# Sums of squares of query, key and head tiles as two float32r matmuls in place of one float32 matmul

## The chip, the cores and the metric

One core of one Trainium2 chip runs the whole program. The metric is the device time of one execution in microseconds. Three runs of the kernel before are given, and one more execution was profiled.

## What is computed

Two layers of a hybrid trunk over 128 context rows and 256 latent rows, 1024 wide. The rows lie side by side as 384 columns on the chip; the model dimension lies on the partitions.

```python
# layer l: x += 0.5*g1*FFN(norm(x)); x += g2*Mixer_l(norm(x)); x += 0.5*g3*FFN(norm(x))
def rmsnorm(x, g):
    return x * lax.rsqrt(jnp.mean(x * x, axis=-1, keepdims=True) + EPS) * g
# even mixer: two-way RG-LRU beside differential attention (4 heads, q and k of 2 x 64)
q = rmsnorm(q.reshape(B, S, 4, 2, 64), q_g);  k = rmsnorm(k.reshape(B, S, 4, 2, 64), k_g)
w = softmax(q0 k0) - lam * softmax(q1 k1)
o = rmsnorm(w @ v, subln_g) * (1 - lam_init)          # over 128 elements of a head
# odd mixer: windowed grouped attention with sinks, 16 query heads, 4 key heads of 64
q = rmsnorm(q.reshape(B, S, 4, 4, 64), q_g);  k = rmsnorm(k.reshape(B, S, 4, 64), k_g)
```

Each `rmsnorm` over a head needs the sum of squares over 64 or 128 partitions of a tile. It is had by a matmul with a constant matrix: `bones` (two blocks of 64 by 64 with 1/64) for q and k tiles, which hold two rows of 64 each, and `ones_h` (1/128 everywhere) for a head of the even mixer.

## The kernel before, in words

A dense product is made of three float32r matmuls per 128x128 weight tile (`mm3`): the high part of the weights with the high and the low part of x, and the low part of the weights with the high part of x, all into one PSUM tile. The weights come in order through SP's queue into `raw`; each is split into `hi` (a copy, as a rule on ACT) and `lo` (a subtraction on DVE), 1024 columns at a time, four deep.

The order of the instructions is written by a small planner. `Clock` keeps a rough time for each engine; the matmul stream (projections, FFN, output projection) is written straight through, and after each matmul `Sched.tick` lets side chains, which are generators, write their next stage when by that clock their inputs are there. A `yield` names the conditions of the next stage: tiles, events, free PSUM banks (`msb`, `scb`, `mmb`), or an engine that is idle (`DVE_IDLE`). Each engine then works through its own list in order. `copy` picks ACT, or DVE where by the clock DVE is done 0.5 us earlier. Constants of this planner (`WIDE_E`, `O_EARLY`, `XN_O` and so on) stay as they are.

A mixer runs in this order. `proj_pass` writes the projection tiles: in the even mixer four `xr` tiles (whose chains feed the RG-LRU scans on DVE), then q, k and v of each of four heads, then four `gt` tiles (gelu gates of the RG-LRU); in the odd mixer twice k, v and four q tiles. Each q or k tile starts `q_chain` or `k_chain`, both through `qk_norm`: square on ACT, a wait for the squares and a PSUM bank, the matmul with `bones`, Ln and Exp on ACT (the inverse root), multiplication on DVE, two DMAs that swap rotary pairs, and the rotation on DVE. `a_chain` makes scores, softmax and transposes for a block of 128 queries, `o_chain` the product with v; in the even mixer `o_chain` then squares its result, sums with `ones_h`, normalises and splits it (`split_out`). Then `out_pass` writes the output projection in two parts of K tiles for each of eight output tiles: in the even mixer first the four heads, then the four RG-LRU tiles; in the odd mixer first K tiles 0 to 2, then 3 to 7. Two PSUM tiles are open at first, two more once all heads are ready. After the last part of an output tile, `update` and `prep` (DVE and ACT) ready it for the next FFN.

Tiles of 384 columns come from one pool, `slab`, of 79. The constants: `cst` holds the cosines, the sines and `bones`, loaded by one DMA from SP's queue at the start; `mixer_consts` is a chain that works out further small constants beside the first FFN.

Of the kernel before, what the change touches and what calls it, by code (L numbers as in the profile page):

```python
# [11 lines left out]
F32 = mybir.dt.float32  # L12
F32R = mybir.dt.float32r
BF16 = mybir.dt.bfloat16
AF = mybir.ActivationFunctionType
ALU = mybir.AluOpType
AX = mybir.AxisListType
PSUM = bass.MemoryType.PSUM

P = 128  # L20
NP_, NS = 128, 256
T = NP_ + NS
# [25 lines left out]
class Event:  # L48
    """Something that a chain of instructions has still to emit, with the tiles that it leaves."""

# [4 lines left out]
class Banks:  # L55
    """PSUM tiles of one tag: how many may be in use at a time, and when the free ones fell free."""

# [4 lines left out]
class Idle:  # L62
    """Ready when an engine has nothing else queued."""

# [18 lines left out]
class Clock:  # L83
    """Rough times of the engines while the program is written: they order the emission and nothing else."""

# [33 lines left out]
class Sched:  # L119
    """Emits the stages of side chains between pieces of the matmul stream, each when its inputs should be there."""  # L120

# [80 lines left out]
class Eng:  # L202
    """An engine's instructions, timed by the clock as they are written."""

# [49 lines left out]
def emit(tc, D, order):  # L254
    nc = tc.nc
    ctx = ExitStack()
    with ctx:
        pool = lambda n, b, **k: ctx.enter_context(tc.tile_pool(name=n, bufs=b, **k))
        cpool = pool("const", 1)
# [10 lines left out]
        clock = sched.clock  # L270
# [51 lines left out]
        def copy(out, in_, scale=None):  # L322
            """out = in_ (times a column), on the engine that should be done with it first."""
            k = {} if scale is None else {"scale": scale}
            r = max(clock.at(in_)[0], clock.at(out)[0])
            ta = max(clock.free["ACT"], r) + S_.cost("activation", out, [in_], k)
            td = max(clock.free["DVE"], r) + V.cost("tensor_copy", out, [in_] if scale is None else [in_, scale], k)
            if td + ON_ACT < ta:
                if scale is None:
                    V.tensor_copy(out, in_)  # L330
                else:
                    V.tensor_scalar(out, in_, scale, None, ALU.mult)
            else:
                act(out, in_, AF.Copy, **k)

# [1 line left out]
        scT = cpool.tile([P, KD, 32], F32, name="scT")  # L337
# [13 lines left out]
        cos, sin = cst[:, 0:256], cst[:, 256:512]  # L351
        bones = cst[:, 512:640]
        ident = cpool.tile([P, P], F32, name="ident")
# [4 lines left out]
        V.memset(ones_d, 1.0 / 1024)  # L358
        ones_h = cpool.tile([P, P], F32, name="ones_h")
        V.memset(ones_h, 1.0 / 128)  # L360
        kc = cpool.tile([P, 4], F32, name="kc")
# [8 lines left out]

# [1 line left out]
        class WS:  # L372
# [70 lines left out]
        def mm(ps, lhsT, rhs, start=True, stop=True):  # L443
            TE.matmul(ps, lhsT=lhsT, rhs=rhs, start=start, stop=stop)
            sched.tick()

# [1 line left out]
        M = {}  # L448
# [27 lines left out]
        def mod_one():  # L476
            """Generator: one modulation tile, a condition per stage."""
            i = mod_at[0]
            l, k, t = mod_todo[i]
            mod_at[0] += 1  # L480
            if t == 0:
                M[l, k] = cpool.tile([P, 8, 2], F32, name=f"M{l}_{k}")
            w = mod_tiles.pop(i)
            for c in range(2):
                yield DVE_IDLE, w
                junk = modp.tile([P, 1024], BF16, tag="junk", name=nm("junk"), bufs=1)
                V.tensor_tensor_reduce(out=junk, in0=w, in1=cbc[:, c, :], scale=1.0, scalar=0.0,
                                       op0=ALU.mult, op1=ALU.add, accum_out=M[l, k][:, t, c:c + 1])
            mod_load()
            if t == 7:  # L490
                mod_finish(l, k)
                mod_done.add((l, k))
# [19 lines left out]

# [1 line left out]
        class XS:  # L514
# [7 lines left out]
        def prep(d, with_sh=True):  # L522
            """Generator: scaled x as two float32r parts, and the sum of squares."""
            q = sl()
            hi = XS.hi[d] = sl(F32R, TB)
            lo = XS.lo[d] = sl(F32R, TB)
            act(q, x[d], AF.Square)
            for r, c in RANGES:
                copy(hi[:, r], x[d][:, r], XS.A[:, d, c:c + 1])
            if with_sh:  # L530
                copy(hi[:, T:TB], XS.sh[:, d, :])
            yield hi, q
            if XS.sq is None:
                XS.sq = q
            else:
                V.tensor_tensor(XS.sq, XS.sq, q, ALU.add)
            for r, c in RANGES:
                V.scalar_tensor_tensor(lo[:, r], x[d][:, r], XS.A[:, d, c:c + 1], r32(hi[:, r]), ALU.mult, ALU.subtract)
            if with_sh:
                V.tensor_tensor(lo[:, T:TB], XS.sh[:, d, :], r32(hi[:, T:TB]), ALU.subtract)  # L540
            sched.fire(XS.ev[d], hi, lo, XS.sq)
# [18 lines left out]
        def normed_all(low):  # L560
            """Starts the chains that leave the normed and modulated x as two float32r parts."""
            xn = [None] * KD
# [37 lines left out]

# [1 line left out]
        def ffn(l, n, nxt):  # L602
# [82 lines left out]

# [1 line left out]
        def evac(ps, direct):  # L687
# [26 lines left out]
        def qk_norm(t, bc, gate, gs):  # L714
            """Generator: leaves the normed rows in t, then returns the two parts of the rotated ones."""
            sq = sl()
            if bc is None:
                act(sq, t, AF.Square)
            else:
                for r, c in RANGES:  # L720
                    act(sq[:, r], t[:, r], AF.Square, bias=bc[:, c:c + 1])
            yield (sq, msb) if gate is None else (sq, msb, gate)
            ps = mst()
            mm(ps[:, :T], bones, sq)
            act(sq, ps[:, :T], AF.Ln, bias=c_eps)
# [16 lines left out]
            V.tensor_tensor(sq[:, 0:NS], sq[:, 0:NS], sin, ALU.mult)  # L742
            return u, sq

        def q_chain(ps, direct, gate, gs, out):
# [77 lines left out]
        def transposed(src, n):  # L823
            """w (128 queries, n*128 keys) -> SBUF (keys, n, queries)."""
            pt = mst()
            for b in range(n):
                TE.transpose(pt[:, b * P:(b + 1) * P], src[:, b * P:(b + 1) * P], ident)
            w = sl()
            copy(w[:, :n * P], pt[:, :n * P])
            free(msb, pt, w)  # L830
            return w
# [15 lines left out]
        def proj_pass(tiles, key, done, low):  # L847
            """Projection tiles in order; the first two share a K order that leaves the last tile of x late."""
            i = 0
# [31 lines left out]
        def out_pass(key, gm, nxt, ready, free_at, early, wide):  # L881
            """Output projection. The K tiles in `early` come first: x takes their part while the others are computed."""
            prep_begin(*nxt)
# [7 lines left out]
            def slot(t, ps):  # L891
                """A bank that has nothing to do: kept while there are units to come."""
                if todo:
                    slots.append((t, ps))
                else:
                    (msb if ps.tensor.name in borrowed else mmb).at.append(t)
# [63 lines left out]

# [1 line left out]
        def even_mixer(nxt):  # L962
# [160 lines left out]
            def o_chain(h):  # L1123
# [12 lines left out]
                free(msb, po, og)  # L1136
                yield sq, msb
                ps = mst()
                mm(ps[:, :T], ones_h, sq)
                act(sq, ps[:, :T], AF.Ln, bias=c_eps)  # L1140
# [29 lines left out]

# [1 line left out]
        def odd_mixer(nxt):  # L1172
# [69 lines left out]

# [1 line left out]
        def wm_load(i):  # L1244
# [5 lines left out]
        def mixer_consts():  # L1250
            yield RS.ev, el, pp
            # differential lambda, negated
            V.tensor_scalar(gsub, par("subln"), 1.0 - LAM_INIT, None, ALU.mult)
            lj = sl()
            for m in range(2):
                V.tensor_tensor_reduce(out=lj[:, 0:64], in0=el[:, 2 * m, :], in1=el[:, 2 * m + 1, :], scale=1.0, scalar=0.0,
                                       op0=ALU.mult, op1=ALU.add, accum_out=ls[:, m:m + 1])
            # -8 * softplus(-lam) on (128, 2 directions, 4 tiles); log1p by its series in z / (2 + z)
            lam = pp[:, PPC["lam"][0]:PPC["lam"][0] + 8]
# [89 lines left out]

# order of the 64 rows of a q or k head on the partitions: the two rows of a rotary pair side by side  # L1350
ROPE = np.array([b + i + s for b in (0, 32) for i in range(16) for s in (0, 16)])
# [135 lines left out]
```

## Time and profile before

| | us |
|---|---|
| median of 3 runs | 1466.14 |
| the runs | 1464.9, 1466.14, 1466.73 |
| the profiled execution, first to last instruction (its span) | 1464.2 |
| PE busy in it | 1436.7 |
| PEld (weight loads, beside PE) | 1398.4 |
| DVE busy | 1115.4 |
| ACT busy | 659.8 |
| POOL busy | 103.8 |

The profiled execution has no other time than its span; the median of the runs is 1.9 us above that. Busy time of PE is modelled to the drain of each matmul, so a short gap between two matmuls does not show in it. The even mixer's matmuls run from about 318 to 482 us, the odd mixer's from about 1042 to 1188 us; the FFNs take the rest.

### The profile page before, as it was taken

To read this page: it belongs to the slowest core of one execution; us is meant where nothing else is said; L and a number is where in the kernel's file an instruction comes from. 1 tells how busy PE (TensorE), PEld (TensorE's weight loads), DVE (VectorE), ACT (ScalarE), POOL (GpSimd) and SP (SyncE) were. 2 spreads that over 40 slices of the span, in tenths; PEclk is the share of its full clock that TensorE was granted. 3 is DMA by queue.
4 is the path that set the end of the run, shared out by engine and by line. 5 is a ranking of instruction groups with operands and counts; after the bars stand their busy time and mean duration, and the time that the engine had idled before them with its cause. 6 is when DMAs were issued, how large, how long until landed. Compare 5 with 4: busy or idle time off the path is not lost.

```text
span 1464.2 us, 21823 instructions
## 1 busy us (share of the span) xinstructions
PE 1436.7 (98%) x8354; PEld 1398.4 (96%) x8354; DVE 1115.4 (76%) x2103; ACT 659.8 (45%) x1193; POOL 103.8 (7%) x214
## 2 busy tenths in 40 slices
PE   4999999999999999999999999999999999999998
PEld 1999999998889999999999999999998899999998
DVE  3899999969998998999979997444698795444332
ACT  3643333348875633333345333333477664333321
POOL 0001111110220011111100110000100000000000
PEclk9999999999999999999999999999999999999999
DMA  9557767652322366766744766333331233333430
GB/s 361 216 185 257 246 245 257 235 173 101 120 99 97 140 230 236 254 243 231 254 177 153 251 243 196 135 119 130 117 107 51 77 120 115 133 126 116 146 135 22
DMA packets 49560, 250.67 MB, mean 171 GB/s; under 512 B 6464, under 2 KB 10960, under 8 KB 28336
## 3 DMA queue, kind: packets, MB, share of 16 engines
q1 hardware_dynamic: 29664, 180.05, 34.0%
q0 software_dynamic: 19792, 69.23, 14.2%
q8 instruction: 66, 1.08, 0.3%
q14 instruction: 38, 0.31, 0.1%
HBM read 244.53 MB, written 2.36 MB: 169 GB/s over the span
## 4 chain that ended last, share of the span: by engine, by line
PE 95%; DMA 2%; DVE 2%; ACT 1%; issue 0%; SPq 0%; DVEq 0%; ACTq 0%
PE sc L214 54%; PE mm L214 36%; PE ms L214 5%; DVE s L214 1%; DMA wm<-in_wm 1%; DMA s<-in_xT 1%; DMA raw<-in_wst 0%; DVE lo L214 0%; ACT s L214 0%; DMA s<-s 0%; ACT hi L214 0%; ACT L317 0%; SPq L737 0%; SPq L1296 0%; DVEq L1434 0%
## 5 line engine op out<-in xcount | busy, mean ns | idle before, releaser
L214 PE MATMUL sc<-s,hi 128*128 128x384 f32 (+1 forms) x2816 | 726.3, 339 | 2.3 <-ACT s L214 1.4
L214 ACT ACTIVATE hi<-raw 128x1024 fp32r<-128x1024 f32 x298 | 315.7, 1060 | 541.7 <-PE sc L214 307.4
L214 DVE TENSOR_TENSOR lo<-raw,hi 128x1024 fp32r<-128x1024 f32 x312 | 381.3, 1223 | 231.2 <-ACT hi L214 230.0
L214 PE MATMUL mm<-s,hi 128*128 128x384 f32 (+1 forms) x2072 | 545.8, 344 | 2.3 <-DVE s L214 2.3
L214 PEld LDWEIGHTS sc<-s,hi 128*128 128x128 f32 x2816 | 512.6, 188 | 5.0 <-ACT s L214 1.8
L214 PE MATMUL sc<-s,lo 128*128 128x384 f32 (+1 forms) x1408 | 475.4, 338 | 0.0
L214 PEld LDWEIGHTS mm<-s,hi 128*128 128x128 f32 x2072 | 372.9, 188 | 12.4 <-issue 3.0
L214 PE MATMUL mm<-s,lo 128*128 128x384 f32 (+1 forms) x1036 | 349.1, 337 | 0.0
L214 DVE CUSTOM_DVE_ANT_0 junk<-wm,cbc 128x1024 bf16<-128x1024 f32 x256 | 312.6, 1221 | 11.0 <-DMA wm<-in_wmt 8.3
L214 PEld LDWEIGHTS sc<-s,lo 128*128 128x128 f32 x1408 | 265.0, 188 | 0.0
L214 PEld LDWEIGHTS mm<-s,lo 128*128 128x128 f32 x1036 | 194.7, 188 | 0.0
L214 ACT ACTIVATE s<-s 128x384 f32<-128x384 f32 (+3 forms) x215 | 108.0, 507 | 171.9 <-DVE s L214 157.0
L214 DVE TENSOR_TENSOR s<-s,s 128x384 fp32r<-128x384 f32 (+6 forms) x214 | 112.0, 528 | 20.0 <-ACT s L214 18.9
L214 POOL DMA_DIRECT2D wm<-in_wmt x126 | 66.6, 528 | 695.1 <-DVE M L214 674.2
L214 DVE SCALAR_TENSOR_TENSOR s<-s,M,s 128x128 fp32r<-128x128 f32 (+3 forms) x256 | 92.4, 416 | 3.8 <-ACT s L214 3.7
L214 ACT ACTIVATE s<-s,M 128x256 fp32r<-128x256 f32 (+1 forms) x167 | 66.3, 446 | 11.0 <-DVE s L214 8.1
L214 DVE SCALAR_TENSOR_TENSOR s<-mm,M,s 128x128 f32<-128x128 f32 x104 | 38.5, 412 | 32.2 <-PE mm L214 32.2
L214 DVE TENSOR_TENSOR s<-sc,s 128x384 f32<-128x384 f32 x106 | 56.8, 551 | 0.0
L214 PE MATMUL sc<-s,s 128*128 128x384 f32 (+2 forms) x208 | 49.0, 373 | 0.7 <-ACT s L214 0.7
L214 ACT ACTIVATE s<-ms 128x384 f32<-128x384 f32 (+3 forms) x80 | 31.8, 423 | 29.8 <-PE ms L214 29.5
L214 PEld LDWEIGHTS sc<-s,s 128*128 128x128 f32 x208 | 34.1, 189 | 7.0 <-ACT s L214 1.3
L214 ACT ACTIVATE s<-sc,sm 128x385 f32<-128x385 f32 (+3 forms) x72 | 35.9, 511 | 0.0
(107 smaller groups left out, 635.1 us busy)
## 6 DMA issues: line engine op xcount, KB each, us to landing
raw<-in_wst SPq DMA_DIRECT2D x156, 1024.0 KB, 5.0
wm<-in_wmt POOLq DMA_DIRECT2D x126, 512.0 KB, 3.8
wm<-in_wm SPq DMA_DIRECT2D x8, 1024.0 KB, 7.6
s<-s SPq DMA_DIRECT2D x36, 64.0 KB, 2.4
s<-in_xT SPq DMA_DIRECT2D x8, 192.0 KB, 7.4
out_y<-s SPq DMA_DIRECT2D x8, 192.0 KB, 1.9
cbc<-in_c_rows SPq DMA_DIRECT2D x1, 1024.0 KB, 8.4
wm<-in_wmt SPq DMA_DIRECT2D x2, 512.0 KB, 9.7
```

Source lines behind the costliest of these rows:

```text
L214: r = fn(*a, **k)
```

## The change

The squares are split into two float32r parts by a new generator, `two_parts`: a copy to float32r and the remainder. Two float32r matmuls into the same PSUM tile, with `bones` or `ones_h` in float32r, take the place of the one float32 matmul. `bones` gets a tile of its own, copied out of `cst` in `mixer_consts`, which therefore also waits for `cst`; `ones_h` is a float32r tile. 1/64 and 1/128 are exact in either type. Comments and docstrings fall away as well.

```diff
-        bones = cst[:, 512:640]
+        bones = cpool.tile([P, P], F32R, name="bones")
...
-        ones_h = cpool.tile([P, P], F32, name="ones_h")
-        V.memset(ones_h, 1.0 / 128)
+        ones_h = cpool.tile([P, P], F32R, name="ones_h")
+        V.memset(r32(ones_h), 1.0 / 128)
...
         def qk_norm(t, bc, gate, gs):
...
-            yield (sq, msb) if gate is None else (sq, msb, gate)
+            parts = yield from two_parts(sq)
+            yield (*parts, msb) if gate is None else (*parts, msb, gate)
             ps = mst()
-            mm(ps[:, :T], bones, sq)
+            for i, part in enumerate(parts):
+                mm(ps[:, :T], bones, part, i == 0, i == 1)
             act(sq, ps[:, :T], AF.Ln, bias=c_eps)
...
+        def two_parts(src):
+
+            hi, lo = sl(F32R), sl(F32R)
+            yield src
+            copy(hi, src)
+            yield hi
+            V.tensor_tensor(lo, src, r32(hi), ALU.subtract)
+            return hi, lo
...
             def o_chain(h):
...
-                yield sq, msb
+                parts = yield from two_parts(sq)
+                yield (*parts, msb)
                 ps = mst()
-                mm(ps[:, :T], ones_h, sq)
+                for i, part in enumerate(parts):
+                    mm(ps[:, :T], ones_h, part, i == 0, i == 1)
...
         def mixer_consts():
-            yield RS.ev, el, pp
+            yield RS.ev, el, pp, cst
+            V.tensor_copy(bones, cst[:, 512:640])
```

## Rows read from the trace of the kernel before

**Rows 1.** The page: busy time of each engine, and the chain that ended last.
```profile
PE 1436.7 (98%) x8354; PEld 1398.4 (96%) x8354; DVE 1115.4 (76%) x2103; ACT 659.8 (45%) x1193; POOL 103.8 (7%) x214
...
PE 95%; DMA 2%; DVE 2%; ACT 1%; issue 0%; SPq 0%; DVEq 0%; ACTq 0%
```

**Rows 2.** Windows: busy time of each engine, granted clock, DMA share and GB/s.
```profile
core 0: us, PE busy (x) PEld busy (x) DVE busy (x) ACT busy (x) POOL busy (x), PEclk, DMA share, GB/s
38.00:318.00 280.00, 280.00 (x1594) 279.70 (x1594) 255.02 (x460) 112.70 (x169) 30.18 (x57) 1.00 0.65 231
318.00:482.00 164.00, 161.62 (x884) 148.01 (x883) 151.83 (x350) 122.98 (x277) 21.69 (x49) 1.00 0.31 105
330.00:431.00 101.00, 101.00 (x542) 89.39 (x540) 97.05 (x211) 81.87 (x190) 21.69 (x49) 1.00 0.32 108
431.00:446.00 15.00, 15.00 (x89) 14.01 (x89) 10.76 (x23) 10.91 (x26) 0.00 (x0) 1.00 0.19 71
1042.00:1188.00 146.00, 144.37 (x1009) 132.72 (x1008) 123.90 (x321) 98.09 (x260) 6.49 (x14) 1.00 0.25 86
```

**Rows 3.** Instructions of two tiles, cst and ones_h; times in ns, starts in us.
```profile
L214 PE MATMUL ms<-s,cst x36: 483/486/590, 355.3 to 1130.2; 128*128 128x384 f32 x36
...
L1305 SPq DMA_DIRECT2D cst<-in_cst x1: 451/451/451, 34.5 to 34.5; - x1
...
DMA to landing us min/median/max: 10.3/10.3/10.3
...
L214 PE MATMUL ms<-s,ones_h x8: 486/486/486, 388.4 to 442.4; 128*128 128x384 f32 x8
```

**Rows 4.** The chain that ended last: start us, us, what.
```profile
350.16 5.30 PE mm L214 x30
...
359.26 0.65 PE ms L214 x2
...
416.08 0.65 PE ms L214 x2
...
484.25 180.97 PE sc L214 x1029
```

**Rows 5.** Groups of instructions by form: busy us, mean ns, idle before.
```profile
L214 DVE TENSOR_TENSOR s<-s,s 128x384 fp32r<-128x384 f32 x100 | 55.5, 555 | 14.8 <-ACT s L214 14.8
L214 ACT ACTIVATE s<-s 128x384 fp32r<-128x384 f32 x99 | 51.6, 523 | 105.9 <-DVE s L214 105.9
```

**Rows 6.** Timeline of ACT, even mixer: start us, us, what, idle before.
```profile
444.85 0.93 ACT L214 ACTIVATE s<-s 128x384 fp32r<-128x384 f32 x2
```

**Rows 7.** Timeline of DVE, end of the even mixer.
```profile
438.63 1.23 DVE L214 TENSOR_TENSOR lo<-raw,hi 128x1024 fp32r<-128x1024 f32 x1 [1.15 <-ACT hi L214]
...
441.71 0.62 DVE L214 TENSOR_SCALAR s<-ms,gsub 128x384 f32<-128x384 f32 x1 [0.95 <-ACT s L214]
444.06 0.56 DVE L214 TENSOR_TENSOR s<-s,s 128x384 f32<-128x384 f32 x1 [1.73 <-ACT s L214]
...
446.46 0.55 DVE L214 TENSOR_TENSOR s<-s,s 128x384 fp32r<-128x384 f32 x1
...
447.32 1.50 DVE L214 TENSOR_TENSOR s<-s,s 128x384 f32<-128x384 f32 x3
448.73 0.74 DVE L214 SCALAR_TENSOR_TENSOR s<-mm,M,s 128x128 f32<-128x128 f32 x2
```

**Rows 8.** Timeline of PE, ACT and DVE, end of the odd mixer's attention.
```profile
1162.74 0.49 ACT L214 ACTIVATE s<-ms 128x384 fp32r<-128x384 f32 x1 [2.19 <-PE ms L214]
...
1163.27 0.56 DVE L214 TENSOR_TENSOR s<-ms,s 128x384 fp32r<-128x384 f32 x1 [2.29 <-ACT s L214]
...
1164.30 0.51 PE L214 MATMUL mm<-s,hi 128*128 128x384 f32 x2
```

**Rows 9.** Timeline of DVE, first FFN.
```profile
36.68 0.22 DVE L214 CAST identb<-ident 128x128 bf16<-128x128 f32 x1
...
52.09 0.15 DVE L214 TENSOR_SCALAR gsub<-pp 128x1 f32<-128x1 f32 x1
```

**Rows 10.** Timeline of PE, even mixer.
```profile
428.21 0.81 PE L214 MATMUL ms<-s,ones_h 128*128 128x384 f32 x2
...
442.04 0.81 PE L214 MATMUL ms<-s,ones_h 128*128 128x384 f32 x2
...
444.26 0.51 PE L214 MATMUL mm<-s,hi 128*128 128x384 f32 x2
...
447.41 0.51 PE L214 MATMUL mm<-s,hi 128*128 128x384 f32 x2
...
481.89 0.45 PE L214 MATMUL sc<-s,hi 128*128 128x386 f32 x1 [0.40 <-DVE s L214]
```

## The prediction

> **What bounds the kernel now.** The page's busy line comes first: PE 98%, PEld (weight loads) 96%, DVE 76%, ACT 45%, and the chain that ended last is 95% PE [rows 1]. So the span is a queue of matmuls, and a shorter matmul anywhere shortens it, unless another engine takes the bound over in that stage. The share of DVE is a mean over stages. The edited lines run only in the two mixers: 318 to 482 us (even) and 1042 to 1188 us (odd). There the windows give PE 161.6 of 164 us and 144.4 of 146, but DVE 151.8 of 164 (93%) and 123.9 of 146 (85%) [rows 2]. Both are nearly full in the even mixer. Between 330 and 431 PE has no idle time and DVE 4 us of 101; between 431 and 446 DVE has 4.2 us of 15 [rows 2]. The granted clock is 1.00 in all of these, and PE is about as busy after, so the clock is no term.
>
> The span is 1464.2 us; the median of the runs is 1466.14, 1.9 above it. The sum is made against the span, and its difference put on the median.
>
> **Removed.** 22 float32 matmuls. Each leaves two records: x36 with the block constant (four heads' q and k in the even mixer, ten tiles in the odd) and x8 with ones_h (four heads) [rows 3]. In the chain of waits such a pair holds PE 0.65 us, while 30 float32r matmuls of the same width take 5.30 us and 1029 take 180.97, 0.176 each [rows 4]. Two of them are 0.35. Each norm thus gives PE back 0.30 us: 12 x 0.30 = 3.6 in the even mixer, 10 x 0.30 = 3.0 in the odd, **6.6 us** in all. No row shows a float32r matmul with these constants; the bounds are nothing saved (0.65, what it takes now) and 0.30, and I take the latter, since 0.176 is shown with every float32r weight. The weight loads keep their number, two per norm. The Trainium skill ("FP8 and Floating Point Precision", TensorE Precision Notes) has a true FP32 matmul make four passes; by that the saving would be two passes, an estimate of 7.7 us in all, but the pairs measure 3.7 times a float32r matmul and not 4.
>
> **Added.** Per norm a copy to float32r and a subtraction. The copy goes to ACT unless the emission's clock finds DVE done 0.5 us earlier; now 99 of the 384-wide float32r copies are on ACT at 523 ns [rows 5], and back to back two take 0.93, so one adds 0.41 [rows 6]. 12 x 0.41 = 5 us on ACT in the even mixer, where it is busy 123 of 164 [rows 2]: nothing by throughput; if ACT were full it would be those 5 us. The subtraction lasts 555 ns [rows 5], but three in a row take 1.41 from the first start to the next instruction's [rows 7]: 0.47 each. That is **5.6 us more on DVE in the even mixer**, 4.7 in the odd. As latency, one norm is 0.52 + 0.56 + two handovers of 0.04 (ACT ends at 1163.23, DVE starts at 1163.27 [rows 8]) - 0.30 = 0.86 us later.
>
> Edits that go together at nothing: ones_h is still one memset; `bones` is one cast of a 128x128 block, some 0.22 us as the cast of the identity, in `mixer_consts`, beside gsub at 52.1 us [rows 9]. It now also waits for cst, issued at 34.5 and landed 10.3 later, at 44.8 [rows 3], so DVE stands for nothing; were it late, the weight remainders queued behind it would be, and PE after them. PE covers the cast: it doesn't stop in 38 to 318 [rows 2]. Each norm takes two more slab tiles, dead after its matmuls; counted from first to last access in program order, no more than 67 of 79 are in use before, so no allocation should wait. The copy needs no activation table.
>
> **What lies on the path.** PE is in order, and the projection's matmuls fill it whatever the norm chains do. The fill ends where the output projection begins, and there the last head counts.
>
> Even mixer: the output projection begins at 444.26; two units of four K steps are open, and six steps without head 3 last until 447.41, where the first step with head 3 stands [rows 10]. Head 3's remainder is written by DVE from 446.46 to 447.01 [rows 7], 0.40 us earlier. With the change PE comes to the end of its six steps 3.6 earlier, at 443.8. Head 3 comes earlier only by what was saved ahead of its own k projection: nine norms, -2.7, since k3's is at 416.1 and head norms at 428.2 and 442.0 follow [rows 4, 10]. Then two lengthened norms, k3's and its own: +1.7. Then what DVE's fuller queue adds between 411 and 444: at least nothing (the 4.2 us idle of 431 to 446 take it), at most 2 us (three more subtractions, 1.4, and some of the scan work that they push back); I take the middle, 1, as no row is nearer to either end. Head 3 is then ready at 447.0 as now (446.0 to 448.0), PE waits some 3.2 us for it, and its step starts at once and not 0.4 later. Of 3.6 us **0.4** is left (-1.4 to +0.6). After it 26 steps (13.7 us) cover the gelu chain as now, and DVE's run from 465.5 to 482 has the same length.
>
> Odd mixer: the first step with the last tile stands at 1164.30, its remainder is done at 1163.83 [rows 8], and two steps without it (1.05 us) come after and could go first. PE comes 3.0 earlier, so its fill ends at 1164.30 + 1.05 - 3.0 = 1162.35. The last tile comes nine norms earlier and one lengthened norm later: -2.7 + 0.86 = -1.84, and with DVE's queue (0 to 1 us; DVE is 85% busy) it is ready at 1162.0 to 1163.0. PE waits 0 to 0.65; I take the middle, 0.35. Of 3.0 some **2.65** is left.
>
> Sum: -0.4 - 2.65 = **-3.05 us**, 1463.1.
>
> **Rivals.** A (the sum above): own range, with its bounds, -4.4 to -1.75: 1461.7 to 1464.4.
>
> B, everything is kept: the last heads come earlier along with PE, because DVE and ACT take the added work in idle time. -6.6, 1459.5. For it: PE hardly stops now although DVE is at 93%. Against: 0.4 us to spare at head 3.
>
> C, slower: DVE sets the end of the even mixer. It would have 151.8 + 5.6 = 157.4 us of work. From the point where over 6.6 of its 12.2 us idle cannot be filled, the stage is longer than 164. If none can, +5.6, and if the odd mixer saves nothing as well, 1471.7. For it: DVE's idle time is in part single waits for these same chains (1.15, 0.95, 1.73 us from 438 to 444 [rows 7]). Against: those waits lie near the projection's end, where pushed-back scan work can go. Also against: in 330 to 482 PE waited for DVE once, 0.40 us at 481.89 [rows 10]. The Trainium skill ("Perfetto Trace Analysis", Identifying the Most-Contended Engine) says to judge TensorE by weight-load occupancy and not by matmul occupancy; here that is 148.0 of 164 [rows 2], under DVE's 151.8, so by this rule DVE is the engine to spare in the even mixer and C is what happens.
>
> D, nothing: the last heads are late in both mixers by as much as PE gained, or float32r costs what float32 did there. 1466.1.
>
> **The numbers.** A 0.44, B 0.20, D 0.23, C 0.13. A measurement of this kernel can tell about 0.2% from no change, 2.9 us. A lies on that line and gives half of its chance to either side: faster 0.23 + 0.20 = 0.43, within 0.21 + 0.23 = 0.44, slower 0.13. The predicted time is A's, 1463.1; the range reaches from B, 1459.5, to the middle of C, 1468.6.
>
> **What would show it.** The pairs with the two constants as single float32r matmuls at 0.176 us; 22 more 384-wide float32r copies and subtractions; DVE near 157 us in the even mixer. A is right if a wait of PE of 2 to 4 us stands where the even mixer's output projection meets head 3, and the odd mixer is 2 to 3 us shorter. B shows both mixers 3 us shorter without new waits. C shows DVE without idle time through the even mixer and PE waiting for it at weight remainders or at its end. Wrong altogether would be a pair that still takes 0.6 us, or a change of over 1 us outside of the two mixers.

## The result, and the profile after

The kernel after takes **1477.17 us** (median of four runs, 1475.19 to 1478.98) against 1466.43 of the kernel before beside it: a ratio of 1.0073, 95% interval [1.0059, 1.0087]. It is 10.7 us slower; the forecast was 3 us faster, and the range ended at 1468.6. The profiled execution took 1477.78, with a span of 1476.0.

The page after, busy time of each engine and the chain that ended last, answers to [rows 1]:

```profile
PE 1435.4 (97%) x8354; PEld 1399.4 (95%) x8354; DVE 1128.1 (76%) x2131; ACT 665.0 (45%) x1210; POOL 103.7 (7%) x214
...
PE 94%; DVE 2%; DMA 2%; ACT 1%; issue 0%; SPq 0%; DVEq 0%; ACTq 0%
```

It hardly differs. The parts of the change are there as drawn up. First the matmuls with the two constants in the kernel after (those of before are in [rows 3]), then its groups by form ([rows 5]):

```profile
L214 PE MATMUL ms<-s,bones x36: 331/338/424, 358.5 to 1130.3; 128*128 128x384 f32 x36
...
L214 PE MATMUL ms<-s,ones_h x8: 337/338/686, 393.4 to 447.8; 128*128 128x384 f32 x8
```

```profile
L214 DVE TENSOR_TENSOR s<-s,s 128x384 fp32r<-128x384 f32 x122 | 67.2, 555 | 15.4 <-ACT s L214 15.4
...
L214 ACT ACTIVATE s<-s 128x384 fp32r<-128x384 f32 x119 | 61.7, 523 | 113.4 <-DVE s L214 112.6 <-issue 0.5
```

A matmul with a constant now shows 338 ns with its drain, the same as any float32r matmul of this width, where each half of a float32 one showed 486. There are 22 more subtractions on DVE. Of the 22 new copies 19 went to ACT and 3 to DVE; one older copy moved from DVE to ACT, so ACT's group grows by 20.

So the loss is a matter of place. Each mixer lies between two norms of x, whose sums use the tile `ones_d`; from the first record of the one sum to the first of the other is the mixer's length. The windows of exactly these stretches, before and then after (columns as in [rows 2]: length, then busy time of PE, PEld, DVE, ACT, POOL, the granted clock):

```profile
320.80:483.40 162.60, 160.22 (x875) 146.61 (x875) 151.01 (x349) 122.96 (x277) 21.69 (x49) 1.00 0.30 105
...
1041.30:1188.00 146.70, 145.07 (x1011) 133.15 (x1011) 123.97 (x321) 98.78 (x261) 6.49 (x14) 1.00 0.25 87
```

```profile
330.00:431.00 101.00, 101.00 (x556) 91.77 (x555) 94.28 (x205) 86.73 (x200) 18.74 (x44) 1.00 0.32 107
431.00:446.00 15.00, 13.45 (x82) 12.52 (x80) 12.99 (x30) 11.54 (x27) 0.56 (x1) 1.00 0.35 122
444.00:457.00 13.00, 5.92 (x18) 4.86 (x18) 12.01 (x27) 8.00 (x14) 0.56 (x1) 0.61 0.18 74
...
320.80:493.50 172.70, 161.82 (x876) 149.35 (x876) 157.77 (x363) 129.36 (x288) 21.55 (x49) 0.96 0.28 99
...
1049.70:1199.40 149.70, 143.59 (x1009) 132.73 (x1008) 129.47 (x332) 101.10 (x269) 6.45 (x14) 1.00 0.24 82
```

The even mixer grew from 162.6 to 172.7, the odd one from 146.7 to 149.7. The start and the FFNs are within 1.2 us each and together 1.3 shorter; they are shorter than in the kernel before in 14 of the 18 runs below too, so that is put down to the profiled execution of before and not to the change. In the even mixer PE is idle for 172.70 - 161.82 = 10.9 us where it was 2.4. Its busy time should have fallen by 3.6, to 156.6, and is 161.8. Of these 5.2 us more some 1.7 are a lower clock (last section); the rest is not broken down, and short gaps between matmuls, which the busy time doesn't show, may be in it. From 330 to 431 it still has no gap [rows 2]; in 431 to 446 DVE is at 13.0 us of 15 where it was at 10.8, and the time goes in 444 to 457, where PE works 5.9 us of 13 and DVE 12.0. In the odd mixer PE works 1.5 us less and idles 4.5 us more.

PE's timeline in that stretch after (start, duration, what, and in brackets how long PE stood and for whom; [rows 10] has the same place before):

```profile
443.67 0.34 PE L214 MATMUL mm<-s,lo 128*128 128x384 f32 x1
445.33 0.44 PE L214 MATMUL ms<-s,ones_h 128*128 128x384 f32 x1 [1.32 <-ACT s L214]
447.77 0.69 PE L214 MATMUL ms<-s,ones_h 128*128 128x384 f32 x1 [2.00 <-DVE s L214]
451.56 0.69 PE L214 MATMUL mm<-s,hi 128*128 128x384 f32 x1 [3.11 <-ACT s L214]
452.90 0.69 PE L214 MATMUL mm<-s,hi 128*128 128x384 f32 x1 [0.65 <-DVE s L214]
...
456.55 0.51 PE L214 MATMUL ms<-s,hi 128*128 128x384 f32 x2
```

And what ACT and DVE did there:

```profile
441.29 1.28 ACT L317 ACT_TABLE_LOAD   x1
442.59 1.76 ACT L214 ACTIVATE s<-s 128x384 f32<-128x384 f32 x4
...
444.76 0.52 ACT L214 ACTIVATE s<-s 128x384 fp32r<-128x384 f32 x1
445.30 1.28 ACT L317 ACT_TABLE_LOAD   x1
448.50 0.58 ACT L214 ACTIVATE s<-ms,kc 128x384 f32<-128x384 f32 x1 [1.92 <-PE ms L214]
...
450.99 0.52 ACT L214 ACTIVATE s<-s 128x384 fp32r<-128x384 f32 x1 [0.53 <-issue]
```

```profile
445.29 3.50 DVE L214 TENSOR_TENSOR s<-s,s 128x384 f32<-128x384 f32 x9
...
449.87 2.97 DVE L214 TENSOR_TENSOR s<-s,s 128x387 f32<-128x387 f32 x7
```

Head 3 is what all wait for. The gelu chain's table load and sigmoids (441.29 to 444.35) now stand ahead of its copy (444.76), so PE stands 1.32 us for the high part; the low part's subtraction is the fifth of the nine on DVE from 445.29, behind four others of 384 columns, 2.00 more; a second load brings the table back for its Ln. The high part of the normed head is copied at 450.99, and its first output projection step starts at 451.56 instead of 447.41; the remainder is the last of the seven on DVE from 449.87, and PE stands 0.65 us more for it. The RG-LRU work on DVE is itself late: of ACT's eight 387-wide Ln, one for a direction of an RG-LRU tile, the last starts 39 us later (before, then after):

```profile
L214 ACT ACTIVATE s<-s,kc x8: 604/614/659, 356.0 to 413.1; 128x387 f32<-128x387 f32 x8
```

```profile
L214 ACT ACTIVATE s<-s,kc x8: 603/608/626, 356.0 to 452.4; 128x387 f32<-128x387 f32 x8
```

The order of the program has changed, not only its speed: the planner was charged with the new instructions.

### The profile page after: what moved, and what is told of

Read it like the earlier page. It is cut to its first block, busy times and chain, and to the rows that moved or that the text cites. A ratio compares the mean times of both kernels' runs of the same rounds, so it can differ in the third digit from the quotient of the medians.

```text
span 1476.0 us, 21860 instructions
## 1 busy us (share of the span) xinstructions
PE 1435.4 (97%) x8354; PEld 1399.4 (95%) x8354; DVE 1128.1 (76%) x2131; ACT 665.0 (45%) x1210; POOL 103.7 (7%) x214
## 4 chain that ended last, share of the span: by engine, by line
PE 94%; DMA 2%; DVE 2%; ACT 1%; issue 0%; SPq 0%; DVEq 0%; ACTq 0%
PE sc L214 53%; PE mm L214 36%; PE ms L214 5%; DVE s L214 1%; ACT s L214 1%; DMA wm<-in_wm 1%; DMA s<-in_xT 1%; DMA raw<-in_wst 0%; DVE lo L214 0%; ACT hi L214 0%; ACT L317 0%; SPq L1310 0%; DVEq L1448 0%; SPq L339 0%; SPq L1259 0%
## 5 line engine op out<-in xcount | busy, mean ns | idle before, releaser
L214 ACT ACTIVATE s<-s 128x384 fp32r<-128x384 f32 (+4 forms) x236 | 117.7, 508 | 182.5 <-DVE s L214 166.3
L214 DVE TENSOR_TENSOR s<-s,s 128x384 fp32r<-128x384 f32 (+6 forms) x236 | 122.7, 530 | 19.0 <-ACT s L214 17.8
```

Of the source, the lines that this page charges most:

```text
L214: r = fn(*a, **k)
```

## The experiments

"Even" and "odd" are the mixers' lengths in the profiled execution, "last Ln" the start of that eighth Ln, counted from the start of the even mixer; all in us. Ratios are to the kernel before, beside which each ran (medians 1465.7 to 1466.6). By the intervals a median is good to some 1.3 to 2.9 us. "Even" carries a chance of its own: in every one of these profiles PE waits 1.98 us for DVE about 6 us into the even mixer, and behind that wait the granted clock fell in e1, e7, e10, e11, e13, e14, e16 and e18 and in no other (last section). That adds 1.5 us: the 20 matmuls from there take 5.16 or 5.17 us in these eight and 3.61 to 3.63 in the others. e7's even mixer has the instructions of the kernel before in their order, and is 1.8 longer.

| run | median | ratio, 95% | even | odd | last Ln |
|---|---|---|---|---|---|
| before | 1466.43 | | 162.6 | 146.7 | 92 |
| after | 1477.17 | 1.0073 [1.0059, 1.0087] | 172.7 | 149.7 | 132 |
| e1_saving | 1460.51 | 0.9966 [0.9957, 0.9976] | 162.8 | 144.2 | 118 |
| e2_work | 1474.75 | 1.0057 [1.0042, 1.0072] | 166.6 | 149.4 | 119 |
| e3_gelu_gate | 1474.54 | 1.0062 [1.0047, 1.0077] | 169.9 | 149.4 | 124 |
| e4_pool | 1473.52 | 1.0055 [1.0038, 1.0072] | 172.7 | 146.3 | 119 |
| e5_lru_now | 1498.72 | 1.0227 [1.0210, 1.0244] | 185.7 | 149.6 | 46 |
| e6_sub_twice | 1485.71 | 1.0136 [1.0121, 1.0151] | 177.7 | 151.9 | 134 |
| e7_odd_only | 1468.38 | 1.0014 [1.0005, 1.0024] | 164.4 | 149.5 | 94 |
| e8_one_part | 1465.55 | 0.9999 [0.9989, 1.0008] | 162.1 | 148.8 | 114 |
| e9_order_alone | 1482.28 | 1.0108 [1.0089, 1.0127] | 175.2 | 152.0 | 134 |
| e10_order_kept | 1480.39 | 1.0096 [1.0076, 1.0116] | 173.2 | 152.1 | 101 |
| e11_order_kept_pool | 1482.82 | 1.0111 [1.0092, 1.0129] | 174.9 | 151.6 | 101 |
| e12_order_kept_one | 1458.61 | 0.9946 [0.9925, 0.9966] | 161.1 | 142.9 | 91 |
| e13_work_no_wait | 1474.59 | 1.0050 [1.0034, 1.0066] | 170.7 | 148.2 | 100 |
| e14_order_later | 1498.38 | 1.0214 [1.0197, 1.0231] | 183.4 | 153.3 | 125 |
| e15_charge_alone | 1480.97 | 1.0101 [1.0086, 1.0116] | 176.3 | 149.8 | 144 |
| e16_no_stand | 1469.80 | 1.0026 [1.0013, 1.0038] | 167.1 | 146.5 | 96 |
| e17_dve_only | 1467.85 | 1.0009 [1.0000, 1.0018] | 165.5 | 145.7 | 94 |
| e18_act_only | 1463.09 | 0.9978 [0.9969, 0.9987] | 163.4 | 144.6 | 94 |

Two theories. **Capacity**: DVE has no room for the subtractions. **Order**: the planner, told of new costs, writes the side chains in an order that is worse. A third comes up later, **latency**: PE stands at a norm's matmul until copy and subtraction are done.

**The two halves of the change.** e1_saving against the kernel after:

```diff
-                act(sq, t, AF.Square)
+                act(part, t, AF.Square)          # part is float32r
...
-            parts = yield from two_parts(sq)
+            parts = part, part
```

> The saving alone: the square is written as float32r by ACT and this one part is used in both float32r matmuls, so no copy and no subtraction is added (the low part is left out and the high part counted twice). DVE capacity theory (the added 10.3 us on DVE are what the change costs): 6.6 us faster than the kernel before, about 1460, both mixers 3 us shorter. Order theory (RG-LRU units that the planner lets in only beside an idle engine are put later as soon as any chain of the mixer moves): the last RG-LRU unit is written later than before, PE waits for it, and less than half of the 6.6 us comes: 1463 to 1467.

e2_work against the kernel after (constants in float32 again):

```diff
-            for i, part in enumerate(parts):
-                mm(ps[:, :T], bones, part, i == 0, i == 1)
+            mm(ps[:, :T], bones, sq)
```

> The added work alone: copy, subtraction and the wait for both parts stay, the sum is one float32 matmul of the squares as before. DVE capacity theory: the full 10.3 us and no saving on PE, 1476 to 1477, with DVE without idle time in the even mixer. Order theory: no table load between the gelu sigmoids and the last head's logarithm here, so less than the change lost: 1469 to 1474, and the even mixer is longer by what the last RG-LRU tile is late.

PE's saving alone gives 5.9 of the 6.6 us forecast, as capacity had it; the added work alone, with its order, costs 8.4, between the two ranges. Both theories live.

**The gelu chain, the scans, POOL, a double subtraction.** e3: gelu's sigmoids wait for head 3's Exp. e4 and e6 against the kernel after:

```diff
-            V.tensor_tensor(lo, src, r32(hi), ALU.subtract)
+            G.tensor_tensor(lo, src, r32(hi), ALU.subtract)    # e4, on POOL
...
             V.tensor_tensor(lo, src, r32(hi), ALU.subtract)
+            V.tensor_tensor(lo, src, r32(hi), ALU.subtract)    # e6
```

e5 takes the idle conditions out of the RG-LRU chain, in eight places, of which one is shown:

```diff
...
-                    yield us[dr], DVE_IDLE
+                    yield us[dr]
...
```

> The changed kernel with one more condition: the gelu sigmoids wait until the last head's Exp is written, so ACT loads the sigmoid table once and not between. Order theory: PE's 7 us of waits at the last head's sum (443.7 to 451.6 us) and the fall of the clock behind them go, the wait for the last RG-LRU tile stays; 3 to 6 us faster than the changed kernel, 1471 to 1474. DVE capacity theory: nothing of DVE's work goes, so the time stays at 1477 within 1.

> The changed kernel with the RG-LRU units written as soon as their inputs are there, without the conditions that ACT or DVE be idle; the work is the same. Order theory: the RG-LRU tiles are done long before the output projection needs them, the even mixer loses most of its 10 us: 1467 to 1471. DVE capacity theory: the same DVE work, the same time, 1476 to 1478; or slower, if the attention chains now stand behind RG-LRU units.

> The changed kernel with the subtraction of the low part on POOL in place of DVE: the same chain, the same or a longer latency of a norm, and none of the 10.3 us on DVE. DVE capacity theory: the cost is gone and the saving on PE stays, 1459 to 1463. Order theory (the later norm alone moves the other chains): most of the loss stays, 1470 to 1475.

> The changed kernel with each of the 22 subtractions done twice on DVE, 10.3 us more of it. DVE capacity theory: both mixers longer by most of that, 1485 to 1488. Order theory: the order of the chains is already spoilt, and 0.47 us more in a norm's latency matters little: 1476 to 1481.

Keeping gelu behind head 3 gives back 2.6 us by the medians (the intervals overlap) and 2.8 in the profiled even mixer, with nearly all else in the order of the kernel after, so gelu's early place is a small part. e5 is a miss: RG-LRU units as early as they can be push the attention chains back, and the even mixer ends at 185.7. Early is no better than late. Doubling the subtraction costs 8.5 us for 22 more of them, as capacity has it; taking it off DVE gives the odd mixer 3.4 us back and the even one nothing, as capacity has not. Neither decides: in both the planner wrote a new order once more (some 680 of the 8354 matmuls in e6 and 450 in e4 stand elsewhere than in the kernel after).

**Where, and with less work.** e7 makes the change in the odd mixer alone; e8 is e1 with one matmul in place of two.

```diff
+            if odd:
+                parts = yield from two_parts(sq)
...
+                mm(ps[:, :T], cst[:, 512:640], sq)      # e7, even mixer as before
...
-            parts = part, part
+            parts = (part,)                             # e8, against e1
```

> The change in the odd mixer alone; the even mixer sums in float32 as before. There are no RG-LRU units and no second table load in the odd mixer, so this is the loss without either. Both theories: the even mixer as before, 162 to 163 us. DVE capacity theory: odd mixer +2 to +4 us, 1468 to 1470. A theory in which only the RG-LRU's order is hurt: odd mixer 2 to 3 us shorter, 1463 to 1464.

> The square is written as float32r by ACT and summed with one float32r matmul; the low part is left out, so nothing is added to any engine and a norm gives PE back 0.65 - 0.176 = 0.47 us, 10.4 us in all. If the mixers are bound by PE: 1456. If DVE and the chains bound the even mixer, as where the saving stood alone: nothing from the even mixer, 3 to 5 us from the odd one, 1459 to 1462.

The odd mixer's loss is its own: 149.5 here too. e8 does less work on PE than any other kernel up to here, nothing more elsewhere, and isn't faster than the kernel before, where its expectation had at least 3 us; that speaks for order. Its own test is e12, below.

**Order and work apart.** In e9 the planner's clock is charged for the change and the instructions are those of before; in e10 to e12 the clock is charged as before and the instructions are new:

```diff
+            clock.run("ACT", S_.cost("activation", hi, [src], {}), [hi], [src])        # e9
...
+            clock.run("DVE", V.cost("tensor_tensor", lo, [src, hi], {}), [lo], [src, hi])
...
             nc.tensor.matmul(out, lhsT=const, rhs=sq, start=True, stop=True)           # e9: float32
...
+            nc.scalar.activation(hi, sq, AF.Copy)                                      # e10
+            nc.vector.tensor_tensor(lo, sq, r32(hi), ALU.subtract)                     # e11: nc.gpsimd
...
+            clock.run("PE", max(T, 128) * 0.00168, [out], [planned, sq])               # e10 to e12
```

> The planner's clock is charged with the two parts and the two float32r matmuls, so that it orders everything around them nearly as it did for the change, but the instructions written for a norm are those of the kernel before: the squares and one float32 matmul, no copy and no subtraction. Nothing of the computation is left out. The work on every engine is that of the kernel before, the order nearly that of the change. Order theory (the planner's new order starts the last RG-LRU units and head 3's norm too late in the even mixer): slower than before, 1472 to 1477, with the even mixer at 168 to 173 against 162.6 and the last RG-LRU tile's Ln later than 120 us into it. DVE capacity theory (the 10.3 us of copies and subtractions are what costs): the time of the kernel before, 1465 to 1467.

> The other corner: the planner is told nothing, so that the order is that of the kernel before, and the copy (on ACT) and the subtraction (on DVE) are written directly behind the squares and the two float32r matmuls in place of the float32 one. Nothing of the computation is left out. Work as in the change, order as before. DVE capacity theory: 1473 to 1477, the even mixer at 170 or more. Order theory: 1460 to 1466, the even mixer at 160 to 164; up to 1 us a norm is possible where DVE stands at the subtraction for ACT's copy, since the two are now written back to back.

> As the run with the order kept, with the subtraction on POOL in place of DVE, so that DVE has no more to do than before and never stands for ACT's copy. Nothing of the computation is left out. DVE capacity theory: 1460 to 1462, since DVE is free of the new work (it was 1473.5 with the planner's own order). Order theory: 1459 to 1466, about the same as the run with the order kept, or better by what DVE stood for the copies there.

> Order of the kernel before, one float32r matmul a norm in place of the float32 one, the squares written as float32r, nothing added: the low part of the squares is left out, so it computes sums that are rounded in their terms. It is the run with one part alone, but with the planner told of the kernel before's costs. Order theory: 1456 to 1459, so about 8 us faster than the 1465.6 of that run with the planner's own order, although both carry the same work. If the order were not what cost there: 1462 to 1466 again.

e9 shows that the order costs by itself: **16.5 us**, without one new instruction in a norm and above the 1472 to 1477 that was expected; the even mixer is 12.6 longer and the odd one 5.3. It is the order of the kernel after: by operation, tile and shape all 8354 matmuls stand in the same order in the two traces, and ACT's and DVE's lists differ only by the copies and subtractions (and the type of `bones`). So the step from e9 to the kernel after is the new instructions alone, in one and the same order, and it is 5.1 us *faster*, 2.5 in the even mixer and 2.3 in the odd one, of 6.6 saved on PE. In the kernel as built the added work costs about 1.5 us, no more than the noise; the order costs more than the whole loss. PE's timeline in e9 shows the same wait for head 3 as in the kernel after:

```profile
447.17 0.91 PE L771 MATMUL ms<-s,ones_h 128*128 128x384 f32 x2 [0.79 <-ACT s L214]
453.44 0.69 PE L214 MATMUL mm<-s,hi 128*128 128x384 f32 x1 [5.35 <-ACT s L214]
454.83 0.69 PE L214 MATMUL mm<-s,hi 128*128 128x384 f32 x1 [0.70 <-DVE s L214]
```

e12 shows it from the other side: the work of e8 in the order of before is 6.9 us faster than e8 (the odd mixer 5.9, the even one 1.0), and **7.2 faster than the kernel before**. PE saves 0.47 us a norm there; of 10 x 0.47 = 4.7 in the odd mixer 3.8 show, of 12 x 0.47 = 5.7 in the even one only 1.5, so there PE's work is not what alone sets the time.

But e10 and e11 are slower too, by 14.6 and 17.1, above the range of either theory: the order of before, which is kept in these runs to the last instruction, does not carry the new work. In it PE's norm matmuls are early in PE's list. First the norms' matmuls in e10 (their line of the program, by tile) and how long, and how often, PE stood before them for whom; then that last part in e11:

```profile
L755 PE MATMUL ms<-s,bones_r x36: 333/438/446, 355.9 to 1142.1; 128*128 128x384 f32 x36
L755 PE MATMUL ms<-s,ones_h x8: 337/338/445, 392.4 to 452.0; 128*128 128x384 f32 x8
its engine sat idle before it (us, times) until:
  DVE s L750: 5.8, 11
  ACT s L749: 2.6, 4
```

```profile
  POOL s L750: 12.5, 17
  ACT s L749: 1.5, 2
```

PE stands 8.4 us at the norms for copies and subtractions in e10, and 14.0 in e11, where POOL's subtraction takes 1039 ns (median) against DVE's 558; so e11 does not test DVE's room. In the kernel after PE stands at no q or k norm, only at head 3's: the planner wrote the matmuls later. That is what its new order buys, and it pays elsewhere.

**What the work costs with the order kept.** e13 keeps e10's instructions, but both matmuls read the squares; e16 lets the subtraction read constants; e17 drops the copy, e18 the subtraction.

```diff
-            return hi, lo
+            return sq, sq                                                              # e13, e16 to e18
...
-            nc.vector.tensor_tensor(lo, r32(sq), r32(hi), ALU.subtract)
+            nc.vector.tensor_tensor(lo, cst[:, 0:T], cst[:, 128:128 + T], ALU.subtract)  # e16, e17
```

> Order of the kernel before, with the copy (ACT) and the subtraction (DVE) written behind the squares exactly as in the run with the order kept, but no matmul waits for them: the squares are written as float32r, and both float32r matmuls of a norm read that tile. So every engine carries the change's work, and PE's wait for the two parts is taken away. The low part is left out of the sums and the high part counts twice. Latency theory (with the order kept it is PE that stands at the norm's matmul until copy and subtraction are done): 1459 to 1462, since PE carries what it carried in the run of the saving alone (1460.5). DVE capacity theory (the 10.3 us on DVE cost by themselves): 1470 to 1480, near the 1480.4 of the run with the order kept.

> The run of the work without the wait, with one thing changed: the subtraction reads two pieces of the constant table in place of the squares and their copy, so that DVE has the same work in the same places and never stands there for ACT (it stood 4.9 us at the 12 subtractions of the even mixer and worked 6.6). The copy on ACT stays. The low part is left out of the sums and the high part counts twice. If it is DVE's standing that costs: 1462 to 1467, the even mixer at 163 to 166. If it is the added work itself: 1470 to 1474, the even mixer at 167 to 170.

> As before it, without the copy on ACT: only the subtractions of constants on DVE are added, 12 in the even mixer (6.6 us) and 10 in the odd one (5.5 us). The low part is left out of the sums and the high part counts twice. DVE capacity theory: the even mixer 4 to 7 longer than the 161 to 162 without them, 165 to 168, total 1465 to 1469. Without any effect of DVE's work: 1459 to 1461.

> The other half: only the copies on ACT are added, 22 of 0.52 us, and no subtraction. The low part is left out of the sums and the high part counts twice. ACT is busy for 123 of 163 us of the even mixer, so by the capacity theory it costs little: 1459 to 1463, the even mixer at 161 to 163. If the 0.5 us that each copy puts ahead of ACT's next instruction (evacuations, softmax) delays the chains: 1464 to 1468.

Latency, with its 1459 to 1462 for e13, was over 12 us off: with nothing waiting for the parts most of the loss stays. The subtractions show why, in e13 and then in e17 (the line below the first is DVE's standing before them; e17 has none): in e13 DVE stands 7.8 us for ACT's copies, besides working 22 x 0.56.

```profile
L751 DVE TENSOR_TENSOR s<-s,s x22: 548/558/560, 357.4 to 1137.2; 128x384 fp32r<-128x384 f32 x22
...
  ACT s L750: 7.8, 9
```

```profile
L750 DVE TENSOR_TENSOR s<-cst x22: 544/550/559, 354.1 to 1130.1; 128x384 fp32r<-128x384 f32 x22
```

Read as a ladder, one step a run (total, then the even mixer alone):

- e18 to e16, the subtractions' work on DVE: +6.7, even +3.7
- e17 to e16, the copies' work on ACT: +2.0, even +1.6 (not shown: within the noise, and the clock fell in e16's even mixer and not in e17's, which makes 1.5)
- e16 to e13, DVE standing for the copies: +4.8, even +3.6
- e13 to e10, PE standing for the parts: +5.8, even +2.5 (in the odd mixer of e10 the clock fell once, in that of e13 never)

The other three steps are larger than their intervals, which are some 2 to 4 us, and in the even mixer they compare runs that all had the fall of the clock behind the first wait. e16, at 1469.8, lies between its two expectations, and its even mixer in that of the added work. e17 and e18 against e12 are +9.2 and +4.5 and hold the second matmul as well, at most 22 x 0.176 = 3.9 of each; if that costs all of its 3.9, the subtractions alone cost 5.3 and the copies 0.6. No run shows it: none has the second matmul in the order of before without copy and subtraction.

**Which part of the charge spoils the order.** e14 (work of e10) moves the squares' ready time, e15 (work of before) charges engine time only:

```diff
+            clock.ready[sq.tensor.name] = (r + 1.6, e)                                 # e14
...
+            clock.run("ACT", S_.cost("activation", hi, [src], {}), [hi], [src])        # e15
+            clock.run("DVE", V.cost("tensor_tensor", lo, [src, hi], {}), [lo], [src, hi])
```

> Work of the change, two parts as in the run with the order kept; the planner is charged no engine time for them, but told that the squares are ready 1.6 us later (copy 0.52, subtraction 0.56 and two waits between engines), so that it writes the norm's matmuls later. Nothing of the computation is left out. In the program's order the last RG-LRU tile's Ln then comes at about 104 us of PE work into the even mixer (87 before, 116 in the change). Latency theory: PE no longer stands at the norms, and the even mixer ends between the order kept (173) and before (163): 165 to 170, total 1466 to 1473. If only the unchanged order is fast and every later norm costs: 1475 to 1483 as with the order kept.

> Instructions of the kernel before (one float32 matmul a norm, no copy, no subtraction; nothing of the computation left out). The planner is charged ACT's copy and DVE's subtraction as engine time and nothing else: the norm's matmul has its old price and its old due time. So it shows what the charge alone does to the order: the RG-LRU units ask for an idle DVE or ACT, and in the program the last tile's Ln comes at 131 us of PE work (87 before), behind a second table load. Order theory with the idle conditions as its mechanism: 1472 to 1482, the even mixer at 168 to 175. If the charge were harmless and only the later norms cost: 1464 to 1468.

The charge on ACT and DVE is enough: 14.5 us without any new work, the last Ln at 144 (in its row, then two places where PE stands for ACT in the same kernel):

```profile
L214 ACT ACTIVATE s<-s,kc x8: 606/620/626, 360.8 to 463.0; 128x387 f32<-128x387 f32 x8
```

```profile
448.66 0.45 PE L214 MATMUL mm<-s,hi 128*128 128x384 f32 x1 [3.14 <-ACT s L214]
...
474.79 1.28 PE L214 MATMUL mm<-s,hi 128*128 128x384 f32 x2 [3.60 <-ACT s L214]
```

e14 is worse than either end of what was expected; its even mixer is 183.4, and the FFN behind it 284.2 where it was 278.8 before (e5's is 284.5). Why a later due time alone does so much harm stays open. Open too is which of the displaced units costs what: the last Ln is late in every slow order that the planner made, but e1 has it at 118 and loses nothing, and e5 has it at 46 and loses most. It marks a changed order and is not shown to be the cause.

## Why the prediction was wrong

- *"Each norm thus gives PE back 0.30 us ... 6.6 us in all"*: right in size. e1 keeps 5.9 of it by the medians, and from e9 to the kernel after 5.1 come through. In e1's profiled execution, 2.3 us above its median, the odd mixer keeps 2.5 of 3.0 and the even one 0 of 3.6, or some 1.3 without the fall of the clock; the sum had 0.4.
- *"5.6 us more on DVE in the even mixer"*: right in size. DVE's work there went from 151.0 to 157.8, forecast 157; 0.7 of it are two copies.
- **The step that failed** is the order that the sum took as given. Head 3 was only shifted along it, and then *"After it 26 steps (13.7 us) cover the gelu chain as now"*. The planner, charged with the new work, wrote another order, and e9 shows what that order costs with the instructions of before: 16.5 us, 12.6 in the even mixer. The prediction had no term for it. Head 3 became ready at 451.5, forecast 446.0 to 448.0, behind a table load, gelu's sigmoids and RG-LRU work that had not been ahead of it. Its other terms were not far off in that order: the new instructions gave 5.1 of 6.6.
- **In the order that it assumed it would have failed as well**, at the step *"Then what DVE's fuller queue adds between 411 and 444: at least nothing (the 4.2 us idle of 431 to 446 take it), at most 2 us"*: with the order kept, e10 is 14.6 us slower. Idle time was taken for room. DVE's 11.6 us idle in the even mixer (12.2 in the longer stretch of [rows 2]) are in the main waits for ACT and PE, 9.5 us in eleven of them, and an engine that works through a list fills them only with what stands in its list just there. The ladder gives the even mixer 3.7 for the subtractions' work, 3.6 for DVE's standing and 2.5 for PE's; the sum had 1 us for DVE's queue and 1.7 for two longer norms, all at head 3.
- These two are not additive: the new order avoids PE's standing at the q and k norms and so meets most of the work's price, at its own. Kept order 173.2 (1.5 of it the clock's fall at 326.6), new order 172.7: either way about 10 us.
- The odd mixer, forecast 2.65 shorter, is 3.0 longer. The head's wait of 0 to 0.65 at its end was the only price looked at. In the kernel after PE stands 6.1 us in it where it stood 1.6, most of it for ACT before transposes and scores; e9's order alone makes the mixer 5.3 longer, e15's 3.1. With the order kept, the ladder there is 1.9, 0.8, 1.7 and 3.9, PE's standing the largest.
- **Rival C** had the direction, at a chance of 0.13, and not the cause. Its price was DVE's work alone in the even mixer and nothing in the odd one, 5.6 in all, and so 1471.7; DVE's standing for ACT, PE's standing for DVE and the order were left out. (The middle of C, from 1466.1 to 1471.7, is 1468.9 and not 1468.6; nothing hangs on it.) The Trainium skill ("Perfetto Trace Analysis", Identifying the Most-Contended Engine) judges TensorE by its weight loads; by that DVE (151.0) stood above PE (146.6) in the even mixer and below it (124.0 to 133.2) in the odd one. The runs with the order kept agree: the subtractions' work costs 3.7 in the even and 1.9 in the odd mixer though nobody waits for it (e18 to e16), and PE's saving in e12 shows as 1.5 of 5.7 in the even and 3.8 of 4.7 in the odd.
- *"the clock is no term"*: nearly right; it was one for some 1.7 us behind the waits at head 3, told at the end.

## What to carry to other kernels

Idle time of an engine that works through a list in order is room only if the new instruction stands in the list where the idle time is; on an engine that is 85 to 93% busy, charge a good part of the new work (here 6.7 of 12.2 us), and add what the engine stands for its operands and what others stand for it. Where a program's order comes from a cost model, a change of costs is a change of order: price it with a run that charges the costs and does the old work, and one that does the new work in the old order. PE's saving was real (5.9 us with two matmuls on one part, 7.2 with one matmul and the order kept), so a form of the two parts that adds no step between the squares and PE is the one to look for.

## What was not expected of the hardware

In 444 to 457 the granted clock of the kernel after was 0.61 on the mean, where it had been 1.00 through the same place before. PE had stood 7.1 us in four waits from 443.7 to 452.9; the 11 matmuls that start from 452.90 to 456.27 then take (456.55 - 452.90) / 11 = 0.33 us each in place of 0.176, about what the lower of the clock's two levels, 1.2 GHz, makes of it, and from 456.55 they are back at the higher. That is 11 x 0.156 = 1.7 us on top of the waits. Such a place costs more than its brackets say.

The same wait does not always do it. PE's wait of 1.98 us at the start of the even mixer is there in all twenty profiles; behind it the granted clock fell to the lower level in eight of them and stayed at the higher in twelve. The stretch with that wait in e16 and then in e17, which differ there in nothing on PE (the column before the last two is the granted clock):

```profile
326.00:332.00 6.00, 4.41 (x16) 4.44 (x17) 5.89 (x24) 2.47 (x6) 0.00 (x0) 0.72 0.00 0
```

```profile
326.00:332.00 6.00, 4.15 (x23) 4.18 (x24) 5.89 (x25) 2.73 (x6) 0.00 (x0) 1.00 0.00 0
```

The first 20 matmuls behind it take 5.17 us in e16 and 3.63 in e17. So two profiles can differ by 1.5 us in one stage though their programs don't differ there, and a step of that size between two runs' stages is not a finding. Why the clock falls behind the same wait in one execution and not in another stays open.
